# Queries and keys of a two-layer trunk: transposed by VectorE blocks and two DMAs through DRAM, in place of TensorE

## The chip, the cores and the metric

The kernel runs on one core of a Trainium2 chip. The metric is the device time of one execution in microseconds (us), the median of a few runs. A core has five engines that run side by side, each with its own in-order queue of instructions: TensorE (PE in the profile, its weight loads PEld), VectorE (DVE), ScalarE (ACT), GpSimd (POOL) and SyncE (SP). An engine that waits at the head of its queue holds everything behind it. DMAs are issued from an engine's queue (here almost all from SP's) and are carried out by 16 DMA engines.

## The reference, cut to what matters

Two decoder layers on 256 tokens of width 2048, in float32. Each layer is x = x + mixer(norm(x)), then x = x + mlp(norm(x)). The mixer of the first layer is causal softmax attention with a forget gate (16 heads of 128), that of the second a mixture of three dilated windows (8 heads, three query/key pairs each, values 256 wide). In both, queries and keys are normed per head before the scores:

```
q = rms_norm(q.reshape(B, S, H, dh), q_gain)
k = rms_norm(k.reshape(B, S, H, dh), k_gain)
...
s = jnp.einsum('bqhd,bkhd->bhqk', q_i, k, preferred_element_type=jnp.float32) * scale
s = s + jnp.transpose(c_i, (0, 2, 1))[..., None] - c_keys[:, :, None, :]
...
p = jax.nn.softmax(s, axis=-1)
return jnp.einsum('bhqk,bkhd->bqhd', p.astype(v.dtype), v)
```

The scores contract over the head dimension, and TensorE contracts over partitions. The projections leave tokens on the partitions, so every normed query and key block of 128 tokens by 128 has to be transposed before its scores.

## The kernel before, in words

**Products.** Every weight matrix is streamed once, in plan order, in pieces of 256 rows by 512 columns ("raw", five buffers). For each piece ScalarE casts it to the rounded form wh (L294) and VectorE computes the remainder wl = raw - wh (L295), five buffers each: a piece's cast waits until TensorE has done with the piece five places earlier. A projection of 512 columns is a `product` (L312): 16 steps k, in each of which TensorE does three matmuls for each of two token tiles (L323, L324, L325) into two PSUM banks. One piece serves two steps. The helper `split` emits load, cast and subtraction of the next piece, after every second step.

**Order.** The order of the side work is written out by hand. `Jobs` keeps generators; each step k of a product is one `tick`. A generator that yields a number is resumed that many ticks later; one that yields a key is resumed when the key is in `jobs.done`. The program's order on each engine follows from where in this sequence an instruction is issued, and the framework adds the waits.

**The mixers' products.** The first layer runs, for j = 0 to 3, a product for four heads' queries ("fq", j), one for their keys ("fk", j) and one for their values ("fv", j). The second runs, for q4 = 0 to 3, three products ("dqk", q4, g) that hold 256 columns of queries and 256 of keys each, and one for values. After each query or key product `qk_chain` (L479) is spawned, 20 chains in all:

- it squares the result out of PSUM (ScalarE, L485, tiles `sq`), sums (VectorE, L489), takes the power -1/2 (GpSimd, L492), and three ticks later scales the result into tiles `qn` (VectorE, L498). `sq` and `qn`, two of each, come from the tag "w", which has five buffers of 128x512;
- four ticks later, for each of the two token tiles, TensorE transposes the four heads' blocks into a PSUM bank (L506, four instructions), and ScalarE and VectorE write the scaled results: the unsplit form of the first token tile (`whole`, L512), and the rounded form and its remainder (L520, L521), one head at a time. The destinations (`heads_pair`) have one buffer each;
- one tick after the second token tile it marks its key as done.

**The heads.** `fox_head` (L665) waits for the keys "fq" and "fk" of its j, then 2*hh + 2 ticks for head hh of four, and issues its scores (L673, L580, L583); softmax, transposes of p and the product with v follow over the next six ticks. `dil_head` (L715) waits for the three "dqk" keys of its q4 and then 4*i + 2 ticks for head i of two.

**Another transpose that is there already.** `transposed_by_dma` (L398) does the same job for the normed x ahead of most products: VectorE transposes the 32x32 blocks of a 128x512 tile (L405), four DMAs on SP's queue write them to a DRAM tile `blocks` (L408), and a fifth on SP's queue reads the tile back with whole rows in place (L410). Seven ticks later ScalarE and VectorE read it (L421, L422).

Of the kernel before, what the change touches and what calls it, by code (L numbers as in the profile page):

```python
# [17 lines left out]
P = 128  # L18
D = 2048
S = 256  # L20
NT = S // P
# [66 lines left out]
def trunk(ctx: ExitStack, tc, x, fox_w_in, fox_b_f, fox_q_gain, fox_k_gain, fox_w_out, dil_w_in,  # L88
          dil_q_gain, dil_k_gain, dil_w_out, mix_norm_g, mlp_norm_g, mlp_w_up, mlp_w_down, out):
    nc = tc.nc  # L90
    jobs = Jobs()
# [15 lines left out]
    ident = const.tile([P, P], F32, name="ident")  # L107
# [14 lines left out]
    gain = const.tile([P, 4 * KC + 8], F32, name="gain")  # L122
# [111 lines left out]
    for q4 in range(4):  # L234
        for g in range(3):
            c = g * DH * P + q4 * 2 * P
# [64 lines left out]
    def in_turn(w, apart=NC // 2):  # L301
        return w.rearrange("p (b h n) -> p b n h", n=apart, h=2)

    def by_column(acc, apart=NC // 2):
        return acc.rearrange("p (b n h) -> p b h n", n=apart, h=2)

    def halves(t, apart=NC // 2):
        return t.rearrange("p (b h n) -> p b h n", n=apart, h=2)
# [167 lines left out]
        return lambda k: (tag, k // 2)  # L476


    def qk_chain(acc, tag, key, parts):  # L479

        yield (tag, "rstd")
        sq = []
        for t in range(NT):
            s = work.tile([P, NC], F32, tag="w", name=f"sq_{key}_{t}", bufs=5)
            nc.scalar.activation(halves(s), by_column(acc[t]), AF.Square, scale=rstd[tag][:, t:t + 1])  # L485
            sq.append(s)
        ss = small.tile([P, NT, 4], F32, tag="ss", name=f"ss_{key}")
        for t in range(NT):
            nc.vector.tensor_reduce(ss[:, t, :], sq[t].rearrange("p (h d) -> p h d", h=4), AX.X, ALU.add)  # L489
        nc.vector.tensor_scalar(ss, ss, 1.0 / P, EPS, ALU.mult, ALU.add)  # L490
        rq = small.tile([P, NT, 4], F32, tag="rq", name=f"rq_{key}")
        nc.gpsimd.tensor_tensor(rq, ss, mhalf.rearrange("p (t h) -> p t h", t=NT), ALU.pow)  # L492
        yield 3
        qn = []
        for t in range(NT):
            nc.vector.tensor_scalar_mul(rq[:, t, :], rq[:, t, :], rstd[tag][:, t:t + 1])
            q = work.tile([P, 4, P], F32, tag="w", name=f"qn_{key}_{t}", bufs=5)
            nc.vector.tensor_mul(q.rearrange("p (h g) d -> p h g d", h=2),  # L498
                                 acc[t].rearrange("p (g d h) -> p h g d", h=2, g=2),
                                 rq[:, t, :].rearrange("p (h g) -> p h g", h=2).unsqueeze(3).to_broadcast([P, 2, 2, P]))  # L500
            qn.append(q)
        yield 4
        for t in range(NT):
            pt = ps_tp.tile([P, 4, P], F32, tag="tp", name=f"ptq_{key}_{t}")
            for h in range(4):
                nc.tensor.transpose(pt[:, h, :], qn[t][:, h, :], ident)  # L506
            for c, nh, gcol, (whole, hi, lo) in parts:
                src = pt[:, c // P:c // P + nh, :]
                gc = gain[:, gcol:gcol + 1]
                keys = hi.shape[2] == S  # L510
                if t == 0:
                    nc.scalar.activation(whole, src, AF.Copy, scale=gc)  # L512
                    if not keys:
                        continue
                at = slice(t * P, (t + 1) * P) if keys else slice(0, P)
                for i in range(nh):

                    order = [x.rearrange("p (h n) -> p h n", h=2) for x in (hi[:, i, at], lo[:, i, at])]
                    of = src[:, i, :].rearrange("p (n h) -> p h n" if keys else "p (h n) -> p h n", h=2)
                    nc.scalar.activation(order[0], of, AF.Copy, scale=gc)  # L520
                    nc.vector.scalar_tensor_tensor(order[1], of, gc, order[0].bitcast(F32), ALU.mult, ALU.subtract)  # L521
            yield 1
        jobs.done.add(key)

    def v_chain(acc, tag, key, dst):
# [139 lines left out]
    def fox_head(j, hh, qT, kT, vt, sel):  # L665
        h = 4 * j + hh
        yield ("fq", j)
        yield ("fk", j)
        yield "gate"
        yield "mask"  # L670
        yield 2 * hh + 2
        ps = ps_sc.tile([P, 512], F32, tag="sc", name=f"sc_f{h}")
        nc.tensor.matmul(ps[:, 0:3 * P], sel[:, hh, :], in_turn(negc, P // 2), start=True, stop=False)  # L673
        for t in range(NT):
            scores(ps, t, qT[hh // 2], kT[hh // 2], hh % 2, True)
        s = work.tile([P, 3 * P], F32, tag="s", name=f"s_f{h}", bufs=4)
# [24 lines left out]
        yield from pv(pt_sb, vt, [hh * P], [hi[:, h % 2, :]], [lo[:, h % 2, :]], f"f{h}")  # L701
        jobs.done.add(("of", h))
# [12 lines left out]
    def dil_head(q4, i, qTs, kTs, vt):  # L715
        h = 2 * q4 + i
        for g in range(3):
            yield ("dqk", q4, g)
        yield 4 * i + 2
        s = work.tile([P, 3, 3 * P], F32, tag="sd", name=f"sd{h}", bufs=1)  # L720
        for g in range(3):
            yield ("table", g)
            ps = ps_sc.tile([P, 512], F32, tag="sc", name=f"sc_d{h}_{g}")
            for t in range(NT):
                scores(ps, t, qTs[g], kTs[g], i)
            slope = 2.0 ** (-8.0 * (g * DH + h + 1) / N_SLOPES)
            nc.vector.scalar_tensor_tensor(s[:, g, :], tables[g], -slope, ps[:, 0:3 * P], ALU.mult, ALU.add)
            yield 1
        nm = small.tile([P, NT], F32, tag="nm", name=f"nm_d{h}")
        den = small.tile([P, NT], F32, tag="den", name=f"den_d{h}")  # L730
        spans = [slice(0, P), slice(P, 3 * P)]
        for t in range(NT):
            nc.vector.tensor_reduce(nm[:, t:t + 1], s[:, :, spans[t]], AX.XY, ALU.max, negate=True)
        yield 1
        for t in range(NT):
            nc.scalar.activation(s[:, :, spans[t]], s[:, :, spans[t]], AF.Exp, bias=nm[:, t:t + 1],
                                 accum_out=den[:, t:t + 1])
        yield 1
        nc.vector.reciprocal(den, den)
# [12 lines left out]
        jobs.done.add(("od", h))  # L752
# [127 lines left out]
    tag = "n0"  # L880
# [58 lines left out]
```

## Time and profile before

| | |
|---|---|
| median of three runs | 2178.54 us (2178.52 to 2178.8) |
| the profiled execution, its own time | 2178.83 us |
| its span in the profile | 2177.1 us |
| TensorE busy | 2168.3 us, 100% of the span |
| VectorE, ScalarE, GpSimd busy | 1386.4, 1107.9, 49.3 us |
| DMA | 435.22 MB, mean 200 GB/s |

The page gives the busy time of each engine, then the span in 40 slices, the DMA queues, the chain of work that ended last, the costliest groups of instructions by line, and the DMAs by line with the time from issue to landing. Views of the trace beside it list who waited for whom, the instructions of one line, and the instructions in order of time. A matmul's row in the trace is longer than the time that it takes from the next, because matmuls overlap; what one costs is read from the distance between starts.

### The profile page before, as it was taken

The page shows a single profiled execution, that of the slowest core. Times are in us where ns is not written, and L with a number is a line of the kernel's source. Part 1 is how long each engine was busy: PE and PEld are TensorE (multiplying, and loading weights), DVE is VectorE, ACT ScalarE, POOL GpSimd, SP SyncE. Part 2 cuts the span into 40 slices and gives each one's busy share as a digit, 9 for nine tenths or more (in the row PEclk, how much of TensorE's full clock was granted, in tenths as well). Part 3 has the DMA queues.
Part 4 walks back from the last instruction along what each step waited for, and adds up shares of the span by engine and source line. Part 5 has one row for each costly group of instructions (what it writes and reads, how often), then busy time and mean ns, then how long its engine had stood idle before and what let it go on. Part 6 is the DMA issues. An engine that isn't in the chain of part 4 may idle for free.

```text
span 2177.1 us, 30019 instructions
## 1 busy us (share of the span) xinstructions
PE 2168.3 (100%) x11392; PEld 1931.3 (89%) x11392; DVE 1386.4 (64%) x1864; ACT 1107.9 (51%) x1553; POOL 49.3 (2%) x52
## 2 busy tenths in 40 slices
PE   9999999999999999999999999999999999999999
PEld 7888888998998998998888888888988988988988
DVE  6776686665665565566676767676655655655564
ACT  6565555544444454455555555555544544544442
POOL 1011000000000000000000000000000000000000
PEclk9999999999999999999999999999999999999999
DMA  7566558666666666667665565667666656656664
GB/s 246 172 185 183 175 175 262 200 203 203 199 202 204 201 202 203 203 202 243 214 190 175 183 191 168 197 200 237 201 203 203 202 203 203 200 202 202 202 211 145
DMA packets 261793, 435.22 MB, mean 200 GB/s; under 512 B 18264, under 2 KB 77200, under 8 KB 261648
## 3 DMA queue, kind: packets, MB, share of 16 engines
q1 hardware_dynamic: 261056, 432.63, 63.0%
q8 instruction: 89, 1.46, 0.3%
q10 hardware_dynamic: 560, 0.66, 0.1%
q14 instruction: 56, 0.46, 0.1%
q0 software_dynamic: 32, 0.02, 0.0%
HBM read 426.42 MB, written 6.82 MB: 199 GB/s over the span
## 4 chain that ended last, share of the span: by engine, by line
PE 98%; DVE 1%; ACT 0%; issue 0%; DMA 0%; POOL 0%; ACTq 0%; POOLq 0%
PE acc L323 21%; PE acc L325 21%; PE acc L324 21%; PE up_n3a_acc L371 5%; PE up_n1a_acc L371 5%; PE up_n3a_sc L371 3%; PE up_n3a_tp L371 3%; PE up_n1a_tp L371 3%; PE up_n1a_sc L371 3%; PE up_n1a_acc L375 3%; PE up_n3a_acc L375 3%; PE up_n1a_sc L375 1%; PE up_n1a_tp L375 1%; PE up_n3a_sc L375 1%; PE up_n3a_tp L375 1%; DVE wl L295 0%
## 5 line engine op out<-in xcount | busy, mean ns | idle before, releaser
L295 DVE TENSOR_TENSOR wl<-raw,wh 128x1024 fp32r<-128x1024 f32 (+1 forms) x801 | 978.6, 1222 | 691.8 <-ACT wh L294 684.4
L294 ACT CAST wh<-raw 128x1024 fp32r<-128x1024 f32 (+1 forms) x801 | 839.0, 1048 | 885.0 <-PE acc L325 528.7
L323 PE MATMUL acc<-wh,hT_n 128*128 128x512 f32 x896 | 346.3, 387 | 0.0
L324 PE MATMUL acc<-wl,hT_n 128*128 128x512 f32 x896 | 340.4, 380 | 0.1
L325 PE MATMUL acc<-wh,hT_n 128*128 128x512 f32 x896 | 340.2, 380 | 0.0
L323 PE MATMUL acc<-wh,aTh_n1a 128*128 128x512 f32 x512 | 194.0, 379 | 0.0
L324 PE MATMUL acc<-wl,aTh_n1a 128*128 128x512 f32 x512 | 194.0, 379 | 0.0
L325 PE MATMUL acc<-wh,aTl_n1a 128*128 128x512 f32 x512 | 194.0, 379 | 0.0
L325 PEld LDWEIGHTS acc<-wh,hT_n 128*128 128x128 f32 x896 | 169.8, 190 | 24.0
L324 PEld LDWEIGHTS acc<-wl,hT_n 128*128 128x128 f32 x896 | 170.1, 190 | 21.4 <-DVE wl L295 0.4
L323 PEld LDWEIGHTS acc<-wh,hT_n 128*128 128x128 f32 x896 | 169.8, 190 | 21.6 <-ACT hT_n L445 0.3
L323 PE MATMUL acc<-wh,aTh_n3a 128*128 128x512 f32 x480 | 181.9, 379 | 0.0
L324 PE MATMUL acc<-wl,aTh_n3a 128*128 128x512 f32 x480 | 181.9, 379 | 0.0
L325 PE MATMUL acc<-wh,aTl_n3a 128*128 128x512 f32 x480 | 181.9, 379 | 0.0
L371 PE MATMUL up_n3a_acc<-hT_n,wh 128*128 128x512 f32 x512 | 181.6, 382 | 0.0
L371 PE MATMUL up_n1a_acc<-hT_n,wh 128*128 128x512 f32 x512 | 181.6, 382 | 0.0
L375 PE MATMUL up_n1a_acc<-hT_n,wl 128*128 128x256 f32 x512 | 139.6, 273 | 0.0
L375 PE MATMUL up_n3a_acc<-hT_n,wl 128*128 128x256 f32 x512 | 139.6, 273 | 0.0
L325 PEld LDWEIGHTS acc<-wh,aTl_n1a 128*128 128x128 f32 x512 | 96.8, 189 | 13.8
L324 PEld LDWEIGHTS acc<-wl,aTh_n1a 128*128 128x128 f32 x512 | 96.8, 189 | 13.7
L323 PEld LDWEIGHTS acc<-wh,aTh_n1a 128*128 128x128 f32 x512 | 96.8, 189 | 13.6
L371 PEld LDWEIGHTS up_n1a_acc<-hT_n,wh 128*128 128x128 f32 x512 | 96.8, 189 | 13.5
(735 smaller groups left out, 3208.4 us busy)
## 6 DMA issues: line engine op xcount, KB each, us to landing
raw<-in_mlp_w_up_dram SPq DMA_DIRECT2D x256, 512.0 KB, 3.8
raw<-in_mlp_w_down_dram SPq DMA_DIRECT2D x256, 512.0 KB, 3.7
raw<-in_dil_w_in_dram SPq DMA_DIRECT2D x192, 256.0 KB, 3.0
raw<-in_fox_w_in_dram SPq DMA_DIRECT2D x95, 512.0 KB, 3.8
raw<-in_fox_w_out_dram SPq DMA_DIRECT2D x32, 512.0 KB, 4.1
raw<-in_dil_w_in_dram SPq DMA_DIRECT2D x32, 512.0 KB, 3.8
raw<-in_dil_w_out_dram SPq DMA_DIRECT2D x32, 512.0 KB, 4.3
blocks_n<-turned_n SPq DMA_DIRECT2D x72, 64.0 KB, 1.9
```

What stands on the lines that cost most here:

```text
L294: issued["cast"] = nc.scalar.copy(hi[:, part, :], raw[:, part, :])
L295: nc.vector.tensor_sub(lo[:, part, :], raw[:, part, :], hi[:, part, :].bitcast(F32))
L323: nc.tensor.matmul(acc[t], ah[:, tok], hi, start=first, stop=False)
L324: nc.tensor.matmul(acc[t], ah[:, tok], lo, start=False, stop=False)
L325: issued["product"] = nc.tensor.matmul(acc[t], al[:, tok], hi, start=False, stop=last)
L371: issued["product"] = nc.tensor.matmul(banks[b], hi[:, i, col], in_turn(tokens.rearrange("p x s -> p (x s)"), P // 2), start=first, stop=last)
L375: nc.tensor.matmul(banks[b][:, 0:S], lo[:, i, col], in_turn(tokens[:, 0, :], P // 2), start=False, stop=False)
```

## The change

All chains but two, ("fk", 3) and ("dqk", 3, 2), no longer use TensorE for the transposes. As soon as a token tile's `qn` is written, VectorE transposes its 32x32 blocks into the `sq` tile, four DMAs on SP's queue write these to a DRAM tile, and one DMA on GpSimd's queue reads them back into the `qn` tile. The chain then waits nine ticks, and two more ahead of each token tile. From the tile in SBUF, ScalarE writes the scaled form, into `whole` for the first token tile and into `sq[0]` for the second (two instructions in a tile, one for each part), and then the rounded form of both heads of a part in one copy; VectorE subtracts. The two chains left as they were keep their four ticks and their code.

The heads are issued further apart: 4*hh + 2 ticks in place of 2*hh + 2 for j = 0 to 2, and 6*i + 2 in place of 4*i + 2 for q4 = 0 to 2.

```
+    by_engine = {("fk", 3), ("dqk", 3, 2)}
...
+        if key in by_engine:
+            yield 4
...
+            jobs.done.add(key)
+            return
+
+        for t in range(NT):
+            turned = sq[t].rearrange("p (j h r) -> p j h r", j=4, h=4)
+            nc.vector.transpose(turned.rearrange("p j h r -> p h j r"),
+                                qn[t].rearrange("p h (j c) -> p h j c", c=32))
+            blocks = dram.tile([4, 32, 4, P], F32, tag="blocks", name=f"blocks_{key}_{t}", bufs=4)
+            for i in range(4):
+                nc.sync.dma_start(blocks[:, :, i, :].rearrange("j c x -> c j x"), sq[t][32 * i:32 * i + 32].rearrange("p (j x) -> p j x", j=4))
+            nc.gpsimd.dma_start(qn[t], blocks.rearrange("j c i x -> (j c) (i x)").rearrange("p (h d) -> p h d", h=4))
+        yield 9
+        for t in range(NT):
+            yield 2
+            for n, (c, nh, gcol, (whole, hi, lo)) in enumerate(parts):
                 keys = hi.shape[2] == S
+                src = qn[t].rearrange("p i (h r) -> p h i r", h=4)[:, c // P:c // P + nh]
+                to = sq[0].rearrange("p (n i x) -> p n i x", n=2, i=2)[:, n] if t else whole
+                nc.scalar.activation(to.rearrange("p h (i r) -> p h i r", i=4), src, AF.Copy, scale=gain[:, gcol:gcol + 1])
+                if t == 0 and not keys:
+                    continue
                 at = slice(t * P, (t + 1) * P) if keys else slice(0, P)
+                a, b = (x[:, :, at].rearrange("p i (h n) -> p i h n", h=2) for x in (hi, lo))
+                of = to.rearrange("p i (n h) -> p i h n" if keys else "p i (h n) -> p i h n", h=2)
+                nc.scalar.copy(a, of)
+                nc.vector.tensor_sub(b, of, a.bitcast(F32))
         jobs.done.add(key)
...
-        yield 2 * hh + 2
+        yield (2 if ("fk", j) in by_engine else 4) * hh + 2
...
-        yield 4 * i + 2
+        yield (4 if ("dqk", q4, 2) in by_engine else 6) * i + 2
```

More of the change, by code (lines that the diff above doesn't have):

```diff
@@ L501, in qk_chain @@
             qn.append(q)
-        yield 4
-        for t in range(NT):
[L504 to L509, printed above, removed]
-                keys = hi.shape[2] == S
[L511 to L514, printed above, removed]
-                at = slice(t * P, (t + 1) * P) if keys else slice(0, P)
[L516 to L522, printed above, removed]
+        if key in by_engine:
+            yield 4
+            for t in range(NT):
+                pt = ps_tp.tile([P, 4, P], F32, tag="tp", name=f"ptq_{key}_{t}")
+                for h in range(4):
+                    nc.tensor.transpose(pt[:, h, :], qn[t][:, h, :], ident)
+                for c, nh, gcol, (whole, hi, lo) in parts:
+                    src = pt[:, c // P:c // P + nh, :]
+                    gc = gain[:, gcol:gcol + 1]
+                    keys = hi.shape[2] == S
+                    if t == 0:
+                        nc.scalar.activation(whole, src, AF.Copy, scale=gc)
+                        if not keys:
+                            continue
+                    at = slice(t * P, (t + 1) * P) if keys else slice(0, P)
+                    for i in range(nh):
+                        order = [x.rearrange("p (h n) -> p h n", h=2) for x in (hi[:, i, at], lo[:, i, at])]
+                        of = src[:, i, :].rearrange("p (n h) -> p h n" if keys else "p (h n) -> p h n", h=2)
+                        nc.scalar.activation(order[0], of, AF.Copy, scale=gc)
+                        nc.vector.scalar_tensor_tensor(order[1], of, gc, order[0].bitcast(F32), ALU.mult, ALU.subtract)
+                yield 1
+            jobs.done.add(key)
+            return
@@ new lines, in qk_chain @@
+        yield 9
+        for t in range(NT):
+            yield 2
+            for n, (c, nh, gcol, (whole, hi, lo)) in enumerate(parts):
+                keys = hi.shape[2] == S
+                src = qn[t].rearrange("p i (h r) -> p h i r", h=4)[:, c // P:c // P + nh]
+                to = sq[0].rearrange("p (n i x) -> p n i x", n=2, i=2)[:, n] if t else whole
+                nc.scalar.activation(to.rearrange("p h (i r) -> p h i r", i=4), src, AF.Copy, scale=gain[:, gcol:gcol + 1])
+                if t == 0 and not keys:
+                    continue
+                at = slice(t * P, (t + 1) * P) if keys else slice(0, P)
+                a, b = (x[:, :, at].rearrange("p i (h n) -> p i h n", h=2) for x in (hi, lo))
+                of = to.rearrange("p i (n h) -> p i h n" if keys else "p i (h n) -> p i h n", h=2)
+                nc.scalar.copy(a, of)
+                nc.vector.tensor_sub(b, of, a.bitcast(F32))
```

## The prediction

> **What bounds the kernel.** I read the profile's page first: engines, clock, DMA, and the chain that ended last.
>
> ```profile
> PE 2168.3 (100%) x11392; PEld 1931.3 (89%) x11392; DVE 1386.4 (64%) x1864; ACT 1107.9 (51%) x1553; POOL 49.3 (2%) x52
> ...
> PEclk9999999999999999999999999999999999999999
> ...
> GB/s 246 172 185 183 175 175 262 200 203 203 199 202 204 201 202 203 203 202 243 214 190 175 183 191 168 197 200 237 201 203 203 202 203 203 200 202 202 202 211 145
> DMA packets 261793, 435.22 MB, mean 200 GB/s; under 512 B 18264, under 2 KB 77200, under 8 KB 261648
> ...
> PE 98%; DVE 1%; ACT 0%; issue 0%; DMA 0%; POOL 0%; ACTq 0%; POOLq 0%
> ```
>
> TensorE is never without work, at full clock, and is 98% of the chain; VectorE and ScalarE have a third and a half of their time free. A busy PE can hide waits, so next the list of what PE waited for, whole:
>
> ```profile
> PE spare L117 <- POOL ident masks.py:199: 2.5, 1, 2.5
> PE ps_g_mix L136 <- DMA g_mix<-in_mix_norm_g_dram: 1.8, 1, 1.8
> PE sc_d L580 <- DVE sd L727: 0.8, 4, 0.2
> PE pc L644 <- DVE g_lf L641: 0.2, 1, 0.2
> ```
>
> After the first microseconds TensorE waits 1.0 us in all. So whatever leaves its queue shortens the time one for one, and every new wait lengthens it.
>
> **What is removed from TensorE.** Transposes in order of time (fence one), and as the chain of waits has them (fence two):
>
> ```profile
> 189.72 0.38 PE L325 MATMUL acc<-wh,hT_n 128*128 128x512 f32 x1
> ...
> 190.37 0.38 PE L325 MATMUL acc<-wh,hT_n 128*128 128x512 f32 x1
> 190.59 0.60 PE L506 MATMUL ptq_('fq', 2)_0_2014<-ident,qn_('fq', 2)_0_1973 128*128 128x128 f32 x4
> ...
> 191.46 0.38 PE L325 MATMUL acc<-wh,hT_n 128*128 128x512 f32 x1
> ```
>
> ```profile
> 214.08 0.44 PE ptq_('fk', 2)_1_2223 L506 x4
> ```
>
> From one L325 to the next is 0.65 us without transposes and 1.09 us with four between them: a set costs 0.44 us, and the chain says the same. There are 8 + 12 = 20 chains of two sets; two chains keep theirs, so 36 sets go: 36 x 0.44 = 15.8 us. All lie on the path. Nothing is added to TensorE; the heads' matmuls only move.
>
> **What is added elsewhere, and its way through the queues.** These rows price the same detour where the kernel already takes it (VectorE blocks, four writes, one read-back), and the one DMA that GpSimd issues today:
>
> ```profile
> L405 DVE STREAM_TRANSPOSE turned_n<-x 128x512 f32<-128x512 f32 x18 | 12.6, 702 | 0.0
> ```
>
> ```profile
> L408 SPq DMA_DIRECT2D blocks_n<-turned_n x72: 303/432/884, 325.3 to 1490.7; - x72
> ...
> DMA to landing us min/median/max: 1.7/1.9/3.3
> ```
>
> ```profile
> DMA to landing us min/median/max: 2.8/4.2/5.5
> ```
>
> ```profile
> g_mix<-in_mix_norm_g_dram POOLq DMA_DIRECT2D x1, 16.0 KB, 4.8
> ```
>
> ```profile
> 1.40 4.84 DMA g_mix<-in_mix_norm_g_dram
> ...
> 13.47 1.24 DVE wl L295
> ```
>
> ```profile
> ACT hT_n L421 <- DMA turned_n<-blocks_n: 3.5, 7, 0.9
> ```
>
> The second landing row is that of the read-back (L410, 18 of them); the last two rows are pieces of the chain (start, length), GpSimd's DMA and the first subtraction of a weight piece. The detour exists 18 times, with seven ticks of time; ScalarE was late at 7 of them, by 0.9 us at most, and TensorE at none. Now one query/key chain of before, ScalarE and then VectorE in order of time:
>
> ```profile
> 1094.89 0.69 ACT L485 ACTIVATE sq_('dqk', 0, 1)_0_10007<-acc,rstd_n 128x512 f32<-128x512 f32 x1 [0.85 <-PE acc L325]
> ...
> 1098.17 1.05 ACT L294 CAST wh<-raw 128x1024 fp32r<-128x1024 f32 x1 [0.96 <-ACT sq_('dqk', 0, 1)_1_10009 L485]
> 1100.76 1.06 ACT L294 CAST wh<-raw 128x1024 fp32r<-128x1024 f32 x1 [1.54 <-PE acc L325]
> ...
> 1105.04 0.47 ACT L512 ACTIVATE dqT_1w<-tq_('dqk', 0, 1)_0_10088,gain 128x256 f32<-128x256 f32 x1 [0.68 <-PE tq_('dqk', 0, 1)_0_10088 L506]
> ...
> 1105.77 0.37 ACT L520 ACTIVATE dkT_1h<-tq_('dqk', 0, 1)_0_10088,gain 128x128 fp32r<-128x128 f32 x1
> ```
>
> ```profile
> 1102.45 0.68 DVE L498 TENSOR_TENSOR qn_('dqk', 0, 1)_1_10048<-acc,rq_('dqk', 0, 1)_10015 128x512 f32<-128x512 f32 x1
> ...
> 1106.17 0.35 DVE L521 SCALAR_TENSOR_TENSOR dkT_1l<-tq_('dqk', 0, 1)_0_10088,gain,dkT_1h 128x128 fp32r<-128x128 f32 x1 [0.55 <-ACT dkT_1h L520]
> ```
>
> Casts, which wait for TensorE, come every 2.59 us: a piece of weights is two ticks, a tick 1.3 us. I count from T = 1094.9, the product's end.
>
> - VectorE: second `qn` written at T+8.2. Two block transposes of 0.70: T+9.0 and T+9.7. Removed: six L521 of 0.35 = 2.1 us; added 1.4 us and three subtractions of 128x256, 0.35 (L521, half the size) to 0.7 (a 128x512 such as L498): 1.0 to 2.1 us. Even, on an engine with 36% free.
> - ScalarE: removed 2 x 0.47 + 6 x 0.37 = 3.2 us; added four of 0.47 and three copies of 0.37 to 0.47: 3.1 to 3.3 us. Nothing.
> - SP: eight writes of 0.43 us: the first four issued by T+10.7, the last beginning at T+10.2, landed T+12.2; the second four issued by T+12.4, landed T+13.9. Behind them on SP stand weight loads:
>
> ```profile
> SPq L273 <- DVE wl L295: 1233.5, 586, 4.4
> ```
>
> ```profile
> L273 SPq DMA_DIRECT2D raw<-in_dil_w_in_dram x224: 367/368/1483, 1031.4 to 1391.9; - x112
> ```
>
> SP waits for a raw buffer at 586 loads, so it is ahead. In the changed kernel's instruction order the writes stand directly behind a load that waits for a subtraction just ahead of the block transposes, so SP reaches them in time, and what follows waits for the next subtraction. Eight writes are 3.5 us; two loads of 0.37 per 2.59 us leave 1.85 us free, so the load behind is about 1.7 us late, against five raw buffers = 13 us. Cost nothing; were that lead gone, 18 x 1.7 = 31 us.
> - GpSimd: two read-backs per chain wait there for the writes. Behind them stand the next chain's power and, in the first layer, the head selectors, ticks away. The read-back's duration R, from issue on GpSimd's queue, is what the trace does not show. Nearest rows: 2.8 to 5.5 us for the same transfer from SP, 4.8 us for a smaller one from GpSimd. I take 4.8, and since nothing in these rows binds it from above in a loaded stretch, carry R along. The Trainium skill, "DMA: Bandwidth & Descriptors", section "Anatomy of one DMA", fits 2.0 us + bytes/436e3 for a DMA from GpSimd: an estimate of 2.6 us here, with which the sum below is the same; the 4.8 us row is longer.
> - DMA traffic: 36 x 512 KB = 18.9 MB, 435 to 454 MB, 210 GB/s over the new time; slices above reach 262. Nothing.
>
> **Where it meets TensorE.** In the changed order the first read of the transposed tile on ScalarE stands behind the cast of the tenth piece after T, which ends at T + 5 x 2.59 + 1.05 = T+14.0. The data is there at T+12.2+R = T+17.0. So ScalarE now waits about 3 us, 18 times, and casts behind it are late by that. Then 1.3 us (two scalings, one copy), a cast of 1.05, 1.7 us for the second token tile, 0.4 for VectorE: done at T+16.6+R = T+21.4. Who is late next:
>
> - First head's scores in layer one (three chains, "fk" 0 to 2): TensorE reaches them at T + 9 x 2.59 = T+23.3. Room for R up to 6.7 us.
> - Third pair's scores in layer two (three chains, "dqk" 0 to 2, 2): T + 10 x 2.59 = T+25.9, R up to 9.3 us.
> - The other 12: TensorE runs out of cast weights at T+25.9, cast and subtraction of the eleventh piece end at T+15.7+R: R up to 10.2 us.
>
> With R = 4.8 TensorE never waits. Heads further apart: no added instruction; their last step is some 36 ticks after the keys' product, and the tiles they hold are written again 46 ticks after it, so nothing waits; the 0.8 us of "sc_d" waits for `sd` (one buffer) may go for three of four pairs: 0 to -0.6 us, taken as 0.
>
> Sum: 2178.83 (the profiled execution, span 2177.1 and 1.7 around it) - 15.8 = 2163.0 us. That execution lies 0.3 us above the median; I predict 2163.0, -0.7%.
>
> **Rivals.**
>
> 1. *Late read-back, heads wait, still faster.* For 6.7 < R < 9.3 each us costs 3 us (three chains): R = 8.5 gives 5.4 us, 2168.4. For it: the single GpSimd DMA took 4.8 us for a sixteenth of the bytes. Against: it ran among the first loads.
> 2. *Starved read-back, slower.* VectorE keeps GpSimd from writing the DMA's descriptors, so R grows to 4.8/(1 - 0.64) = 13.3 us if it can only work in VectorE's gaps. Cost: 3 x 6.6 + 3 x 4.0 + 12 x 3.1 = 69 us: 2232. It decides from R = 10.35: there 3 x 3.65 + 3 x 1.05 + 12 x 0.15 = 15.9 us equals the gain. The Trainium skill, "SBUF — State Buffer", section "SBUF: two separate sides", states it: a DMA issued from GpSimd stalls while VectorE holds the port that both share (620 ns alone, about 3100 ns beside a copy, says its next section). Its section "Who interferes with whom" narrows it to copies, casts and tensor_scalar operations and, by inference, frees subtractions of two tensors. What runs on VectorE between T+12 and T+17 is almost only these subtractions (L295), so I hold it unlikely; no trace here shows it, since the one GpSimd DMA of before was over at 6.2 us, ahead of the first subtraction at 13.5.
> 3. *The removal is worth nothing*: weights become the bound and the time stays, 2178. Against: casts wait for TensorE (the 1.54 in the 1100.76 row) and SP for buffers. What it needs is a queue that falls behind by more than five buffers.
>
> **How the numbers follow.** Forecast (TensorE without new waits of note, 2161 to 2166): 0.60. Rival 1 and kindred small waits, 2166 to 2174: 0.17. Rival 3, or waits that just eat the gain, 2174 to 2183: 0.06. Rival 2 and its kin (SP's lead gone, 2194): 0.17. A measurement of this kernel tells about 0.2% (4.4 us) from no change, so faster is below 2174.2: 0.77; same 0.06; slower 0.17. The range goes from 2160 (all of the gain, the 0.6 us, and some 2 us of reading error in 36 x 0.44) to 2180, which takes in rival 1 whole and part of rival 3 and leaves out 0.2. The likeliest case's own range is 2161 to 2166.
>
> **What would show it.** Right: TensorE's transposes of `qn` fall from 160 to 16, its list of waits stays near 5 us, ScalarE's first scaling of each chain waits 2 to 4 us for the read-back, landing in about 5 us, and the granted clock stays full. Wrong: the list of PE's waits gains "sc_f" or "sc_d" rows released by ScalarE or VectorE, or wh and wl rows behind that scaling, with read-backs of 7 us and more; or SP's loads land late. What would make the prediction wrong is R above 6.7 us, or a tick count that I misread.

## The result and the profile after

The changed kernel takes 2198.0 us (median, 2196.5 to 2203.1) against 2178.5 us for the kernel before: a ratio of 1.0093, interval 1.0078 to 1.0108. It is slower by 0.9%; 2163.0 us was predicted. The profiled execution took 2197.98 us, with a span of 2196.3 us.

The profile's page of the changed kernel: busy time by engine, the DMA total, and the shares of the chain that ended last.

```profile
PE 2159.9 (98%) x11248; PEld 1920.0 (87%) x11248; DVE 1396.1 (64%) x1847; ACT 1105.5 (50%) x1536; POOL 69.4 (3%) x88
...
DMA packets 285412, 454.12 MB, mean 207 GB/s; under 512 B 21144, under 2 KB 98512, under 8 KB 285264
...
PE 81%; DVE 5%; DMA 4%; issue 4%; ACT 2%; SPq 1%; POOL 1%; ACTq 0%; DVEq 0%; POOLq 0%
```

The 144 matmuls (36 sets of four) are gone, but TensorE's busy time fell by 8.4 us only, and its idle time rose from 8.8 us (2177.1 - 2168.3) to 36.4 us. 27.6 - 8.4 = 19.2 us, the growth of the span. What TensorE waits for (in total, times, longest):

```profile
PE sc_d L612 <- DVE sd L759: 16.3, 4, 6.7
PE po_f L578 <- DVE pTl_f L591: 4.9, 3, 1.6
PE ptp_f L586 <- DVE s_f L724: 2.6, 3, 1.3
...
PE tq_('dqk', 3, 2)_0_12877 L510 <- DVE qn_('dqk', 3, 2)_0_12836 L501: 1.5, 1, 1.5
```

The rows that are new or grew by over 1 us are heads, and one pair that TensorE still transposes; weights stay a small item (0.4 us). Where the time is lost can be read from the output products of the two mixers. One line adds them to x, in layer one first (start of the row) and in layer two last (end of the row): L775 before, L807 after.

```profile
L775 DVE TENSOR_TENSOR x<-x,acc x16: 679/680/682, 323.4 to 1505.9; 128x512 f32<-128x512 f32 x16
```

```profile
L807 DVE TENSOR_TENSOR x<-x,acc x16: 680/680/684, 328.5 to 1524.3; 128x512 f32<-128x512 f32 x16
```

Layer one ends 5.1 us later, and the stretch from there to the last addition (the rest of layer one, without chains, and the mixer of layer two) grows from 1182.5 to 1195.8 us, by 13.3 us. Behind it 0.8 us are added.

The mechanism stands in ScalarE's order of time. Of the three chains of the first group of layer two, these are the first square (L488), the fifth cast behind the second square (L294), and the first scaling of the tile that was read back (L546), each with the idle time ahead of it:

```profile
1078.60 0.69 ACT L488 ACTIVATE sq_('dqk', 0, 0)_0_9815<-acc,rstd_n 128x512 f32<-128x512 f32 x1 [0.91 <-PE acc L325]
...
1092.14 1.05 ACT L294 CAST wh<-raw 128x1024 fp32r<-128x1024 f32 x1 [1.54 <-PE acc L325]
1095.67 0.51 ACT L546 ACTIVATE dqT_0w<-qn_('dqk', 0, 0)_0_9853,gain 128x256 f32<-128x256 f32 x1 [2.49 <-DMA qn_('dqk', 0, 0)_0_9853<-cks_('dqk', 0, 0)_0_9859]
...
1098.88 0.91 ACT L546 ACTIVATE sq_('dqk', 0, 0)_0_9815<-qn_('dqk', 0, 0)_1_9856,gain 128x256 f32<-128x256 f32 x2 [0.81 <-issue]
...
1101.37 0.68 ACT L488 ACTIVATE sq_('dqk', 0, 1)_0_10009<-acc,rstd_n 128x512 f32<-128x512 f32 x1
...
1112.86 1.05 ACT L294 CAST wh<-raw 128x1024 fp32r<-128x1024 f32 x1 [1.54 <-PE acc L325]
1119.86 0.51 ACT L546 ACTIVATE dqT_1w<-qn_('dqk', 0, 1)_0_10047,gain 128x256 f32<-128x256 f32 x1 [5.95 <-DMA qn_('dqk', 0, 1)_0_10047<-ks_('dqk', 0, 1)_0_10053]
...
1125.79 0.68 ACT L488 ACTIVATE sq_('dqk', 0, 2)_0_10198<-acc,rstd_n 128x512 f32<-128x512 f32 x1
...
1133.58 1.05 ACT L294 CAST wh<-raw 128x1024 fp32r<-128x1024 f32 x1 [1.54 <-DVE wl L295]
1144.15 0.51 ACT L546 ACTIVATE dqT_2w<-qn_('dqk', 0, 2)_0_10238,gain 128x256 f32<-128x256 f32 x1 [9.52 <-DMA qn_('dqk', 0, 2)_0_10238<-ks_('dqk', 0, 2)_0_10244]
```

The fifth casts go by TensorE's pace: 20.7 us apart, a product's length. The first scalings go by the chain: 24.2 and 24.3 us apart. So the wait grows by some 3.5 us from chain to chain, 2.49, 5.95, 9.52. It is a loop: squares, detour (17.1 to 18.5 us to the first scaling), second scaling (1098.88), one cast, and only then the next chain's squares. One round takes 22.8 us, the next 24.4, where TensorE leaves 20.7. The third squares are 1125.79 - 1078.60 - 41.4 = 5.8 us late.

At the end TensorE's score of the third pair waits. VectorE and then TensorE in order of time:

```profile
1150.17 0.42 DVE L554 TENSOR_TENSOR dkT_2l<-sq_('dqk', 0, 2)_0_10198,dkT_2h 128x256 fp32r<-128x256 f32 x1
...
1152.24 0.74 DVE L562 SCALAR_TENSOR_TENSOR dv0l<-acc,rstd_n,dv0h 128x512 fp32r<-128x512 f32 x1
...
1154.03 0.55 DVE L759 SCALAR_TENSOR_TENSOR sd<-dist,sc_d 128x384 f32<-128x384 f32 x1
```

```profile
1147.67 0.38 PE L325 MATMUL acc<-wh,hT_n 128*128 128x512 f32 x1
1154.73 0.77 PE L612 MATMUL sc_d<-dkT_2w,dqT_2w 128*128 128x128 f32 x2 [6.68 <-DVE sd L759]
...
1155.93 0.63 PE L323 MATMUL acc<-wh,hT_n 128*128 128x512 f32 x1
1156.36 0.63 PE L324 MATMUL acc<-wl,hT_n 128*128 128x512 f32 x1
...
1159.16 0.38 PE L325 MATMUL acc<-wh,hT_n 128*128 128x512 f32 x1
1159.38 0.38 PE L323 MATMUL acc<-wh,hT_n 128*128 128x512 f32 x1
```

The chain's last subtraction ends at 1150.6; VectorE then works off what stood behind it (two weight pieces, the values) before L759 frees the bank that the score needs. This L759 reads the first pair's scores, which TensorE had done by 1145; only VectorE's order kept it. So 2.5 of the 6.68 us pass before the chain's end and 4.1 behind it. And the stall costs more than its 6.68 us: matmuls start 0.43 us apart until 1159, where 0.22 is normal. By stretches (busy times; then the granted clock, DMA share, GB/s):

```profile
1152.00:1155.00 3.00, 0.27 (x1) 0.30 (x2) 3.00 (x5) 3.00 (x4) 0.00 (x0) 0.52 0.49 154
1155.00:1159.00 4.00, 4.00 (x13) 3.37 (x13) 4.00 (x6) 0.69 (x3) 0.00 (x0) 0.50 0.81 256
1159.00:1163.00 4.00, 4.00 (x22) 3.54 (x21) 1.89 (x4) 2.19 (x5) 0.00 (x0) 1.00 0.47 153
```

The clock fell to a half about 4 us into the stall and stayed so for some 4 us of work, which costs about 2 us. The third group has the same picture (a stall of 5.67 us, matmuls at 0.43 us until 1350), so some 4 us of the busy time are this.

Layer one loses its time in another way. These are VectorE's rows, and then TensorE's, where the last head of j = 1 meets the query chain of j = 2:

```profile
186.64 0.17 DVE L493 TENSOR_SCALAR ss_('fq', 2)_1923<-ss_('fq', 2)_1923 128x8 f32<-128x8 f32 x1
188.60 0.23 DVE L499 TENSOR_SCALAR rq_('fq', 2)_1927<-rq_('fq', 2)_1927,rstd_n 128x4 f32<-128x4 f32 x1 [1.78 <-POOL rq_('fq', 2)_1927 L495]
188.74 1.22 DVE L295 TENSOR_TENSOR wl<-raw,wh 128x1024 fp32r<-128x1024 f32 x1
189.87 0.42 DVE L591 TENSOR_TENSOR pTl_f<-ptp_f,pTh_f 128x256 fp32r<-128x256 f32 x1
```

```profile
190.34 0.38 PE L578 MATMUL po_f<-pTl_f,fv1h 128*128 128x256 f32 x1 [1.63 <-DVE pTl_f L591]
```

The head's `pTl_f` stands on VectorE behind the next query chain, which waits 1.78 us there for GpSimd's power. The same happens at 118.8 and 262.6, 1.63 us each: the 4.9 us of the list. In the kernel before VectorE has no work of a head in this stretch. The chain's end is later (16 ticks behind its product in place of 9) and the heads are further apart, so the last head of a group falls on the next group's query chain.

### The profile page after: what moved, and what is told of

It reads as the page before. It is cut to its first block, busy times and chain, and to the rows that moved or that the text cites. A ratio compares the mean times of both kernels' runs of the same rounds, so it can differ in the third digit from the quotient of the medians.

```text
span 2196.3 us, 30101 instructions
## 1 busy us (share of the span) xinstructions
PE 2159.9 (98%) x11248; PEld 1920.0 (87%) x11248; DVE 1396.1 (64%) x1847; ACT 1105.5 (50%) x1536; POOL 69.4 (3%) x88
## 4 chain that ended last, share of the span: by engine, by line
PE 81%; DVE 5%; DMA 4%; issue 4%; ACT 2%; SPq 1%; POOL 1%; ACTq 0%; DVEq 0%; POOLq 0%
PE acc L323 16%; PE acc L324 16%; PE acc L325 16%; PE up_n3a_acc L371 5%; PE up_n1a_acc L371 5%; DVE wl L295 3%; PE up_n3a_sc L371 3%; PE up_n3a_tp L371 3%; PE up_n1a_tp L371 3%; PE up_n1a_sc L371 3%; PE up_n1a_acc L375 3%; PE up_n3a_acc L375 3%; ACT wh L294 2%; PE up_n1a_sc L375 1%; PE up_n3a_sc L375 1%
## 5 line engine op out<-in xcount | busy, mean ns | idle before, releaser
L294 ACT CAST wh<-raw 128x1024 fp32r<-128x1024 f32 (+1 forms) x801 | 836.5, 1046 | 858.7 <-PE acc L325 505.5
L324 PEld LDWEIGHTS acc<-wl,hT_n 128*128 128x128 f32 x896 | 170.9, 191 | 24.3 <-DVE wl L295 2.3
L325 PEld LDWEIGHTS acc<-wh,hT_n 128*128 128x128 f32 x896 | 170.3, 190 | 24.4
L371 PEld LDWEIGHTS up_n1a_acc<-hT_n,wh 128*128 128x128 f32 x512 | 96.8, 189 | 13.5
```

The costliest lines, as they stand in the source:

```text
L294: issued["cast"] = nc.scalar.copy(hi[:, part, :], raw[:, part, :])
L324: nc.tensor.matmul(acc[t], ah[:, tok], lo, start=False, stop=False)
L325: issued["product"] = nc.tensor.matmul(acc[t], al[:, tok], hi, start=False, stop=last)
L371: issued["product"] = nc.tensor.matmul(banks[b], hi[:, i, col], in_turn(tokens.rearrange("p x s -> p (x s)"), P // 2), start=first, stop=last)
```

## The experiments

All against runs of the kernel before on the same chip. Theory A is the loop above; its rivals are named in the expectations. A count in them is to be corrected: they speak of four (six) casts between the squares and the first scaling of the changed kernel (of e5), and the traces show five (seven) behind the second square.

**e1 and e2: one layer at a time.**

```
-    by_engine = {("fk", 3), ("dqk", 3, 2)}
+    by_engine = {("fk", 3)} | {("dqk", q, g) for q in range(4) for g in range(3)}
```

```
-    by_engine = {("fk", 3), ("dqk", 3, 2)}
+    by_engine = {("dqk", 3, 2)} | {(x, j) for x in ("fq", "fk") for j in range(4)}
```

> Only the seven chains of layer one take the detour; all twelve of layer two are transposed by TensorE and their heads stand as before. Theory A (lateness carried: ScalarE waits in order for a read-back, the next chain's squares start late, and TensorE meets the sum at a head's scores): the loss arises stage by stage. In the changed kernel the last value product of layer one is reached at 302.4 us against 297.1, so this stage alone costs 5.3 us net: 2178.5 + 5.3 = 2184 us, and the 6.7 us waits at L612 are gone. Theory B (the added transfers and the eight writes per chain on SP slow the weight loads): the loss goes with the number of chains, 7 of 18 of 19.4 us = 7.5: 2186 us, with waits for wh and wl spread over layer one.

> Only the eleven chains of layer two take the detour; layer one is transposed by TensorE. Theory A: the stage of layer two costs 18.2 - 5.3 = 12.9 us net (last value product at 1435.7 against 1417.5 us): 2178.5 + 12.9 = 2191 us, three waits of about 6 us at L612 and two stretches of halved clock. Theory B: 11 of 18 of 19.4 = 11.9: 2190 us. The two runs together must add up to the changed kernel's loss if the stages don't act on each other.

Measured: e1 2183.0 us (ratio 1.0020, 1.0011 to 1.0029), e2 2192.8 us (1.0061, 1.0044 to 1.0077). The losses, 4.2 and 13.9 us, add up to 18.1 of the 19.4: each layer makes its own. Both theories gave nearly the same numbers here, so these runs locate the loss and do not tell its cause; but TensorE's waits for wh and wl, which theory B named, are 0.2 us in e1.

**e4: the detour beside the transposes.** Block transposes, writes and read-backs are made for 18 chains, and TensorE transposes as before; what is computed from is TensorE's.

```
-        if key in by_engine:
-            yield 4
+        if key not in by_engine:
+            for t in range(NT):
+                turned = sq[t].rearrange("p (j h r) -> p j h r", j=4, h=4)
+                nc.vector.transpose(turned.rearrange("p j h r -> p h j r"),
+                                    qn[t].rearrange("p h (j c) -> p h j c", c=32))
...
+                nc.gpsimd.dma_start(sq[t], blocks.rearrange("j c i x -> (j c) (i x)"))
+        if True:
+            yield 4
```

> TensorE transposes all chains as before, and the detour is made beside it for 18 chains: block transposes on VectorE, eight writes on SP, two read-backs on GpSimd, whose data nobody reads. Heads stand as far apart as in the changed kernel. Theory A: nobody waits for the read-back, so 2178 to 2181 us (25 us of block transposes lie in VectorE's idle third). Theory B: the loss of 19.4 + 15.8 = 35 us that the detour caused stays, and the transposes stay too: 2178.5 + 35 = 2213 us.

Measured: 2179.2 us, ratio 1.0002 (0.9992 to 1.0011), and TensorE's longest wait behind the first microseconds is 0.8 us. 18.9 MB more traffic, eight writes per chain on SP, 36 block transposes, 36 DMAs on GpSimd and heads further apart cost nothing together. Theory B is out: what costs comes with computing from the data that was read back. One part e4 does not test: its key chains still end after 9 ticks, so the heads, though further apart, are done before the next query chain's waits (the last `pTl_f` of j = 1 starts at 176.1 us, against 189.9 in the changed kernel).

**e3: the scalings two ticks later in the program.**

```
-        yield 9
+        yield 11
...
-                to = sq[0].rearrange("p (n i x) -> p n i x", n=2, i=2)[:, n] if t else whole
+                to = qn[0].rearrange("p (n i) x -> p n i x", n=2)[:, n] if t else whole
```

> The same detour for the same 18 chains, but ScalarE's two scalings stand two ticks later in its order (16 and 18 after the product's end, the second one behind the next chain's squares; its scratch is the first qn tile, so that the squares' buffers do not wait for it). Theory A: ScalarE then waits for a read-back 1 us or less, no lateness is carried to the next squares, L612 waits are gone; transposes off the path give 2178.5 - 15.8 = 2163 us, up to 2168 with small waits left. Theory B: traffic and queues are unchanged, so about 2198 us again.

Measured: 2193.7 us, ratio 1.0067 (1.0052 to 1.0082). Inconclusive on the theory, since the edit did not do what it says: in layer two ScalarE still has five casts between the second square and the first scaling, and the second scaling still stands ahead of the next squares. The ticks do not set an engine's order alone; the framework had moved the scalings ahead of casts that come earlier in the program (held behind the newest cast of its tick, in e5, the changed kernel's scaling stands behind seven). (The section on the kernel before tells only the first half of this.) A place in an engine's queue must be read from the trace, and held by an explicit edge.

**e5 and e6: the scalings held behind casts.** e5 is the changed kernel with this, e6 is e3 with this:

```
-                nc.scalar.activation(to.rearrange("p h (i r) -> p h i r", i=4), src, AF.Copy, scale=gain[:, gcol:gcol + 1])
+                with behind(issued["cast"]):
+                    nc.scalar.activation(to.rearrange("p h (i r) -> p h i r", i=4), src, AF.Copy, scale=gain[:, gcol:gcol + 1])
```

> The changed kernel with one edit: on ScalarE each scaling of a read-back tile is held behind the newest cast of its tick, so that it stands behind six casts after the squares in place of four. Nothing else moves (e3 had moved the ticks alone, and ScalarE's order had kept the scaling behind the same number of casts, so it had not tested this). Theory A (ScalarE's place in order: it stops for data that come at T+18 while casts that are ready stand behind, and the lateness is carried into the next squares): ScalarE's waits at L546 fall from up to 9.5 us to under 2, the waits at L612 go, 2163 to 2168 us. Theory C (the detour, 18 us from the squares to the data and 22 to the end of the chain, is too long for the heads wherever ScalarE reads it): the waits of TensorE stay at L612, at 2190 us or more.

> As e5, with the scalings two ticks later (behind eight casts), the second one behind the next chain's squares and with its scratch in the first qn tile. Theory A: no wait at L546 at all, but the chain ends 2.6 us later, so that the first scores come close: 2163 to 2172 us. Theory C: the heads wait 2.6 us longer than in e5 at each of their six gates.

Measured: e5 2172.7 us, ratio 0.9972 (0.9961 to 0.9983); e6 2169.6 us, 0.9958 (0.9943 to 0.9973). With the same DMAs and the same landing (5.3 us at the median in e6) ScalarE waits for no read-back any more, and "sc_d" is back at 0.2 us. e6, TensorE's waits:

```profile
PE po_f L579 <- DVE pTl_f L592: 3.9, 3, 1.3
...
PE sc_d L613 <- DVE sd L760: 0.2, 1, 0.2
```

In layer two theory C, that the detour is too long for the heads wherever it is read, is out; in layer one the waits for `pTl_f` stay. e5 is nearly 5 us above the upper end expected for it, and the table below shows that layer one is where it falls short.

**e12: only the second scaling held.** As e6, with the condition `if t`: the first scaling stays five casts behind its squares.

```
+                with behind(*([issued["cast"]] if t else [])):
```

> As e6, but only the second scaling of a chain is held, behind both of the next chain's squares; the first stays four casts behind its own squares, where ScalarE waits for the read-back. This parts two readings of e6. If the loop is what costs (squares, detour, second scaling, next squares: 22.8 and 24.4 us round in the changed kernel, against a product's 20.7), the waits at the first scaling stay, but no longer grow: 2 to 3 us in the first, second and third pair alike (2.5, 5.9, 9.5 in the changed kernel), no wait at L612 above 1 us, 2169 to 2174 us. If each wait of ScalarE costs by itself, with the casts behind it, L612 keeps waits of several us and the time stays at 2185 us or more.

Measured: 2169.6 us, ratio 0.9956 (0.9940 to 0.9973), as e6. ScalarE in order of time, first squares and first scalings of the same group:

```profile
1076.21 0.69 ACT L488 ACTIVATE sq_('dqk', 0, 0)_0_9815<-acc,rstd_n 128x512 f32<-128x512 f32 x1 [0.91 <-PE acc L325]
...
1093.00 0.51 ACT L547 ACTIVATE dqT_0w<-qn_('dqk', 0, 0)_0_9853,gain 128x256 f32<-128x256 f32 x1 [2.21 <-DMA qn_('dqk', 0, 0)_0_9853<-cks_('dqk', 0, 0)_0_9859]
...
1096.87 0.69 ACT L488 ACTIVATE sq_('dqk', 0, 1)_0_10003<-acc,rstd_n 128x512 f32<-128x512 f32 x1 [0.49 <-PE acc L325]
...
1116.41 0.51 ACT L547 ACTIVATE dqT_1w<-qn_('dqk', 0, 1)_0_10047,gain 128x256 f32<-128x256 f32 x1 [4.90 <-DMA qn_('dqk', 0, 1)_0_10047<-ks_('dqk', 0, 1)_0_10053]
...
1119.67 0.68 ACT L488 ACTIVATE sq_('dqk', 0, 2)_0_10192<-acc,rstd_n 128x512 f32<-128x512 f32 x1
...
1137.82 0.51 ACT L547 ACTIVATE dqT_2w<-qn_('dqk', 0, 2)_0_10238,gain 128x256 f32<-128x256 f32 x1 [5.58 <-DMA qn_('dqk', 0, 2)_0_10238<-ks_('dqk', 0, 2)_0_10244]
```

The second squares come 20.7 us behind the first, on time, and the third 22.8 behind those: 2.0 us late in place of 5.8. ScalarE still idles at every read-back, more than expected (up to 5.6 us), but beyond this group the wait no longer grows from chain to chain: it is 4.4, 3.2 and 3.7 us in the second group and 5.0, 2.7 and 3.7 in the third, where the changed kernel has 1.8, 4.6, 7.1 and 2.0, 3.4, 9.3. It costs TensorE nothing at the third pairs (0.2 us at L613). e3 is the same kernel without the hold, scratch buffer and ticks included, so the hold alone is worth 2193.7 - 2169.6 = 24.1 us. By the table below 22.7 us of it lie in layer two (1193.9 to 1171.2); layer one ends no earlier (325.2 and 326.1). In layer two, then, ScalarE's idle time is not the price; the second scaling's place ahead of the next squares is.

**e7: heads four ticks later**, in both layers; the chains are as in the changed kernel.

```
-        yield (2 if ("fk", j) in by_engine else 4) * hh + 2
+        yield (2 if ("fk", j) in by_engine else 4) * hh + 6
...
-        yield (4 if ("dqk", q4, 2) in by_engine else 6) * i + 2
+        yield (4 if ("dqk", q4, 2) in by_engine else 6) * i + 6
```

> The changed kernel with every head's first step four ticks (5.2 us) later; chains and ScalarE's order as they were. If TensorE meets the lateness at the heads' scores only, the 16.3 us at L612 and the 4 us of halved clock behind them go, and most of the 9 us in layer one: 2168 to 2178 us. If the late casts would have stopped TensorE anyway (weights), waits for wh and wl take their place and the time stays above 2190 us.

Measured: 2179.5 us, ratio 1.0003 (0.9993 to 1.0012): 1.5 us above the first case, far below the second. ScalarE's waits stay (8.4 and 7.7 us in the first group), "sc_d" falls from 16.3 to 1.4 us, and small waits for wl and wh come up, 3.1 us in all. TensorE meets the lateness at the heads' scores first, and at the weights next.

**e8: the detour only for chains that no head waits for last.**

```
+    by_engine = {("fk", j) for j in range(4)} | {("dqk", q, 2) for q in range(4)}
```

> The detour only for 12 chains that are not the last before a head: queries in layer one, the first and second pair in layer two; keys and third pairs are transposed by TensorE, heads as close as before. 24 sets of transposes go: 2178.5 - 10.6 = 2168 us if nothing waits. Theory A: ScalarE still waits in the first and second pair (2 and 6 us), so the third pair's squares and transposes come late by some of it: 2168 to 2176 us. Theory C (each detour has its price, 35 us for 18): 2168 + 23 = 2191 us.

Measured: 2196.3 us, ratio 1.0081 (1.0066 to 1.0096), outside theory A's 2168 to 2176, and nearer to the 2191 of theory C, which e6 rules out in layer two. With two thirds of the chains nearly the whole loss is back. TensorE's waits show the way:

```profile
PE tq_('dqk', 3, 2)_0_12883 L510 <- DVE qn_('dqk', 3, 2)_0_12842 L501: 4.0, 1, 4.0
...
PE tq_('dqk', 2, 2)_0_12017 L510 <- DVE qn_('dqk', 2, 2)_0_11976 L501: 2.1, 1, 2.1
```

The third pair's squares are late from the two chains ahead of it, and TensorE now needs its `qn` within seven ticks of the product's end, earlier than any score. The loop predicts the direction; I had put the gate in the wrong place. The span grew by 17.4 us: TensorE is idle for 19.5 us more than before (28.3 against 8.8), and the 24 sets take 10.6 us off. The clock was a half not only around the stall of 4.0 us, but behind shorter ones too. These are the stretches around the 2.1 us wait of the second row, in the columns of the fence on the stall above:

```profile
1317.00:1319.40 2.40, 0.26 (x3) 0.03 (x1) 1.03 (x4) 0.67 (x1) 1.33 (x1) 1.00 0.68 217
1319.40:1320.60 1.20, 1.20 (x8) 1.12 (x9) 1.20 (x2) 0.53 (x2) 0.00 (x0) 1.00 0.00 0
1320.60:1324.00 3.40, 3.40 (x12) 2.75 (x11) 3.40 (x5) 2.00 (x5) 0.00 (x0) 0.50 0.59 184
```

In all TensorE worked for some 12 us at half clock in e8, which costs about 6 (the last section tells when the clock falls). That leaves some 2.5 us of the 17.4 without a cause.

**e10: the read-back on SP's queue.**

```
-            nc.gpsimd.dma_start(qn[t], blocks.rearrange("j c i x -> (j c) (i x)").rearrange("p (h d) -> p h d", h=4))
+            nc.sync.dma_start(qn[t], blocks.rearrange("j c i x -> (j c) (i x)").rearrange("p (h d) -> p h d", h=4))
```

> The changed kernel with the read-back on SP's queue in place of GpSimd's; ScalarE's order as before (four casts between the squares and the first scaling). Theory G (GpSimd's queue is what makes the data late): the landing falls from 5.3 to the 4.2 us of the older read-backs on SP, and the loss of 19 us goes with it: 2180 us or less. Theory A (ScalarE's place is four casts behind the squares, ahead of data that come at T+18): 1 us less is carried over per chain, so the waits at L612 shrink from 16 to some 10 us, but stay: 2185 to 2195 us; and SP stands for two waits of 2 to 3 us per chain ahead of weight loads, which its lead covers.

Measured: 2184.6 us (2180.2 to 2186.6), ratio 1.0027 (1.0018 to 1.0036): 0.4 us under theory A's range and 4.6 above theory G's. The landing is 4.1 us at the median, against this of the changed kernel on GpSimd's queue:

```profile
DMA to landing us min/median/max: 3.0/5.3/6.5
```

ScalarE's waits in the second and third chain are 3.5 and 5.9 us (5.9 and 9.5 with GpSimd), and the waits at L612 fall from 16.3 to 5.7 us, so the loop is there, a little faster. (These rows are of an execution of 2180.2 us, the fastest of the ten.) By the medians, 1.2 us less of landing go with 13.4 us less of time: in a loop a delay counts again in every round. So the queue accounts for 13.4 of the 19.4 us. It makes the loss larger, and does not make it alone: the kernel is still slower than before, and e6 gains on GpSimd's queue.

**e9 and e11: the parts put together.** e9 is e6 with e7's heads; e11 has layer one as in e7 and layer two as in e6.

```
-        yield 11
+        yield 11 if key[0] == "dqk" else 9
...
+                with behind(*([issued["cast"]] if key[0] == "dqk" else [])):
...
-        yield (2 if ("fk", j) in by_engine else 4) * hh + 2
+        yield (2 if ("fk", j) in by_engine else 4) * hh + 6
```

> e6 with every head's first step four ticks later, as in e7. In e6 layer two has all of its gain (270.5 us from the first value product to the last, against 277.2 before), but layer one none (the last value product at 298.3 us against 297.1 before, where seven chains without transposes should have given 290.9), with three waits of TensorE for pTl_f and VectorE's work crowded around the heads. If the heads' place is what costs there, 2169.6 - 4 to 7 = 2163 to 2166 us; if it is something else (weights late in layer one), 2169 us again.

> Layer one as in e7 (scalings where the changed kernel has them, heads four ticks later), layer two as in e6 (scalings held behind eight casts, heads as in the changed kernel). Counted to the first and the last addition of the two mixers' output products, e7 gained 3.7 us in layer one (319.7 against 323.4) and e6 11.3 us in layer two (1171.2 against 1182.5 between the two). If the stages don't act on each other, as e1 and e2 add up, 2178.5 - 3.7 - 11.3 = 2163.5 us. If e6's layer two depends on what layer one hands it (late weights, SP's lead), 2167 us or more.

Measured: e9 2172.6 us, ratio 0.9973 (0.9962 to 0.9983), a miss; e11 2164.8 us, 0.9940 (0.9926 to 0.9953), 1.3 us from what the two stages gave. The first and last additions to x, as in the rows above, from the profiled execution of each (us):

| kernel | first | first to last | median time |
|---|---|---|---|
| before | 323.4 | 1182.5 | 2178.5 |
| changed | 328.5 | 1195.8 | 2198.0 |
| e1 layer one | 326.5 | 1182.7 | 2183.0 |
| e2 layer two | 323.9 | 1196.2 | 2192.8 |
| e3 later ticks | 325.2 | 1193.9 | 2193.7 |
| e4 unread | 324.0 | 1182.4 | 2179.2 |
| e5 hold | 326.6 | 1173.3 | 2172.7 |
| e6 hold later | 324.4 | 1171.2 | 2169.6 |
| e7 heads later | 319.7 | 1187.2 | 2179.5 |
| e8 no gate | 325.9 | 1197.4 | 2196.3 |
| e9 hold, heads | 322.8 | 1176.3 | 2172.6 |
| e10 read on SP | 326.9 | 1180.1 | 2184.6 |
| e11 mixed | 319.6 | 1171.6 | 2164.8 |
| e12 second only | 326.1 | 1171.2 | 2169.6 |

Later heads help layer one and hurt layer two (e9: 1176.3 against 1171.2, with 3.5 us of new waits for `p_d`), so what I had read from e7 held for one layer only. Holding the scalings gives layer two 11 us; in layer one it leaves waits for `pTl_f`. e11, TensorE's waits:

```profile
PE spare L117 <- POOL ident masks.py:199: 2.5, 1, 2.5
PE ps_g_mix L136 <- DMA g_mix<-in_mix_norm_g_dram: 1.8, 1, 1.8
PE pc L677 <- DVE g_lf L674: 1.1, 1, 1.1
PE ptp_f L587 <- DVE s_f L725: 1.1, 3, 0.5
...
```

That is near the list of before (7.5 us in all against 5.3), and the waits for `pTl_f` are gone. e11 beats both kernels.

## Why the prediction was wrong

- **The removal, 15.8 us, one for one: right.** Where nothing stalls, TensorE's busy time falls by 2168.3 - 2153.3 = 15.0 us (e6) and by 17.0 (e11), and e11's time lies 1.8 us above the 2163.0 predicted.
- **DMA traffic, SP's writes, the block transposes on VectorE: nothing. Right**, by e4. SP's lead held.
- **Heads further apart: nothing. Wrong in layer one.** The prediction looked at the heads' instructions and tiles, and not at VectorE's queue: there the last head, late from the longer chain and the wider spacing together, stands behind the next query chain, 3 x 1.63 = 4.9 us.
- **R, 4.8 us: right in size.** 5.3 us at the median, 6.5 at most, under the 6.7 that was called room. The starved read-back (rival 2) did not come: GpSimd's DMA instructions take 0.54 to 0.61 us each beside VectorE's subtractions. The Trainium skill, "SBUF — State Buffer", section "Who interferes with whom", lets subtractions of two tensors contend with GpSimd's reads only; the trace shows no sign of a stall of its DMAs.
- **The first scaling waits 2 to 4 us: about right at the first chain of a group alone.** The data came 17.1 us behind the squares, as summed (T+17.0). In layer two the first chains wait 1.6 to 2.5 us, the second 3.4 to 5.9, the third 7.1 to 9.5.
- **The step that failed is "Where it meets TensorE".** It counted each chain from its own T, as if every chain began on time, and compared one chain's end (T+21.4) with the rooms (T+23.3, T+25.9). It did not ask what stands behind the second scaling on ScalarE: the next chain's squares. The prediction's own times, with the order of the trace, show it. Data at T+17.0, 1.3 us of scalings, a cast, 1.7 us for the second tile and one more cast make T+22.1 for the next squares, and the product takes 20.7. So a group's second chain begins 1.4 us late, the third 2.8; measured were 2.1 and 5.8. e12 shows that in layer two this place is the cause: with the second scaling behind the next squares, and the waits for the read-backs left, 24 us go. The step also took the chain's end for the last thing that a score waits for; in the stall of 6.68 us it was a bank, which VectorE freed 4.1 us after the chain's end.
- **A stall priced one for one: too low.** Around the stalls of 6.7 and 5.7 us the clock was a half, which costs some 4 us of busy time in all.
- **Two slips change nothing.** ScalarE's addition has a lower end of 3.0 us, not 3.1. And the subtraction at 13.5 us is the first on the chain that ended last; VectorE's first of a weight piece starts at 6.9 us, which is still behind the end of the GpSimd DMA at 6.2.
- **What stays open.** The span grew by 27.6 us of idle time less 8.4 of busy time. Of the 6.6 us between 8.4 and e6's 15.0, the clock explains about 4; some 2 are not assigned, which is no more than the busy time differs among e6, e11 and e12 (15.0, 17.0 and 13.5 us below that of before). In layer one the changed kernel loses 5.1 us and the 6.2 of seven chains' transposes; the waits for `pTl_f` and `s_f` are 7.5 of these 11.3 us. Holding the scalings does not move the heads, and e6 keeps 1.3 us at each of the three places; moving them (e7, e11) clears these. Why e9, with both, keeps 4.0 us of them, and why e11 gains 3.8 us there and not 6.2, is not settled; nor is what is left of e8.
- **The rivals.** None had the mechanism. Rival 1 came nearest, as its place (scores of the third pair and of layer one's heads) is where TensorE met the lateness; but it made it depend on R above 6.7 us, and put it on the faster side.

## What to carry to other kernels

When a step of a repeated chain is given a longer way, follow ScalarE's (or any in-order engine's) queue round to the same step of the next chain, and compare one round with the time that the bounding engine takes for it: a round that is longer by 2 us is not 2 us of slack used, but 2 us more at every turn. If the work that waits can be put behind the next chain's start, the latency may stay as it is (e12). Read an instruction's place from the engine's order in the trace, not from where the program issues it, and hold it there by an edge if it matters (e3 against e6). And work that is moved later falls on what comes next: look at who else uses each engine's queue there (the heads of layer one).

## What the runs showed of the hardware that I had not expected

- TensorE's clock changes on a beat. In the changed kernel it was a half from 1152.14 to 1158.96 us and from 1343.28 to 1350.11; in e8 for 3.41, 3.41 and 6.83 us from 1218.23, 1320.63 and 1416.20. Within each run all of these times lie whole multiples of 3.413 us apart (56 and 58; 30, 31, 58 and 60). The beat decides what a stall does. The 2.1 us up to 1319.38 in e8 lay inside one beat and halved the clock for the next, when TensorE was busy again; the 3.1 us up to 1249.24 in the changed kernel were shared by two beats (one ends at 1247.7), 1.5 us in each, and the clock stayed at 1.00. The least that halved it was 1.9 us of idle time in a beat (e8, ahead of 1218.23). The Trainium skill, "TensorE: Matmul & The Clock Gate", Part 1, states a free-running window of about 3.4 us, after which an idle TensorE falls to half rate; the trace agrees with the window, and here it did not have to be idle throughout.
- A read-back of 256 KB took 5.3 us (median) from GpSimd's queue and 4.1 us from SP's (e10), beside the same weight loads.
